# Alternating the two heads' 64-row products on TensorE, and another order of its pieces

## The chip, the cores and the metric

The kernel runs on one core of a Trainium2 chip. The metric is device time in microseconds (us) of one execution, the median of several runs. The core's engines are TensorE (PE in the profile, with its weight loads as PEld), VectorE (DVE), ScalarE (ACT), GpSimd (POOL) and SyncE (SP), which issues most DMAs.

## What is computed

One block on 512 tokens of width 1024: an RWKV-7 time mixer and a Mamba-2 (SSD) mixer side by side on one normed input, a gated merge, an output projection, and a mixture of 32 experts, two per token. Cut to its calls:

```python
h = rmsnorm(x, attn_norm_g[l])
proj = h @ w_in[l]
y_a = rwkv7_mix(p_rwkv, ...)    # 16 heads of 64, state 64x64 a head, scanned over tokens
y_b = ssd_mix(p_ssd, ...)       # 32 heads, chunks of 64
merged = g_a * (y_a @ w_up_rwkv[l]) + g_b * (y_b @ w_up_ssd[l])
x = x + merged @ w_out[l]
x = x + hier_moe(rmsnorm(x, ffn_norm_g[l]), ...)
return rmsnorm(x, final_norm_g)
```

The part that the change touches is inside `rwkv7_mix`, whose recurrence for one head is

```python
sa = jnp.einsum('bhij,bhj->bhi', state, -kk_t)
state = state * w_t[:, :, None, :] + sa[..., None] * (kk_t * a_t)[:, :, None, :] + v_t[..., None] * k_t[:, :, None, :]
y_t = jnp.einsum('bhij,bhj->bhi', state, r_t)
```

## The kernel before

The channels lie on the partitions, the 512 tokens along the free axis. The recurrence is computed in 8 chunks of 64 tokens, for two heads at a time: a *pair* has head 0 on partitions 0 to 63 and head 1 on 64 to 127. There are 8 pairs (`HP`).

Two phases come before the experts. In each, several *streams* (Python generators) are advanced by the function `drive` (line 266), which reads a string of the table `PLAN`: a letter advances one stream to its next `yield`, a number n issues n *pieces* of projections from a queue. A piece (lines 150 to 152) is three products of 128 rows by 512 columns; 8 pieces make one 128-column tile of the input projection. A tile's weights are split on their way into a high half (`wh`, ScalarE) and a low half (`wl`, VectorE, line 135), after a DMA from SyncE's queue; two tiles of each are held. TensorE's instructions stand in the program in the order in which these calls issue them, so the table fixes TensorE's order. The other engines' orders come from a scheduler that sees the same program.

The streams of the first phase are: a and b, the chains over chunks of even and odd pairs (`rwkv_chain`); c, their ends (`rwkv_tail`); d, a 32 by 32 inverse for each chunk (`rwkv_inverse`, 62 small VectorE instructions, lines 528 and 529, and TensorE pieces at lines 538, 550 and 560); e, what makes a pair's operands (`rwkv_front`); f, steps of the SSD. The second phase has one stream, the SSD's groups of heads (`ssd`), and the same kind of queue.

`rwkv_front` of one pair, as far as the change goes:

- Line 403 and 404: decay and `a` of the pair, each one product over 128 rows (`zst`) and one over 64 rows (`zlo`), into the banks `psw` and `psa`.
- Lines 475 to 481: GpSimd and VectorE make `LL` and `BK`, the left and right factors, a third of each for either head.
- Lines 486 to 502: for each head and each half of the chunks, four products of 64 rows by 128 columns into one bank, then three VectorE instructions (499 to 501) that mask them into `NB`, `LL` and `RB`, then a `yield`: four steps.
- Lines 504 to 511: for each head, eight transposes of 64 rows into one bank, one copy by ScalarE, a `yield`: two steps.

All these banks come from a ring of three (`rtile`, tag `rot`), which the other streams use too. A step that asks for a bank waits until the bank's last reader is done. The products are float32; each shows as two records in the trace, a transpose as one. A projection's products are float32r and show as one.

Behind the phases come the output projection, the router and the 32 experts, with 192 weight transfers of 1 MB each (6 an expert) through 18 buffers, which become free as the phases' pools close.

Of the kernel before, what the change touches and what calls it, by code (L numbers as in the profile page):

```python
# [14 lines left out]
AF = mybir.ActivationFunctionType  # L15
# [7 lines left out]
C = 64  # L23
NCK = T // C
# [15 lines left out]


PLAN = (
    "abcdef15e3e4e2e2e3e11e2e1e10ee8e1e2e1e1e1e1edeee4e1e2e2e2ee12ee9ee1e1dde1ddea1e1aedeee1ae3e1ae2e1a1ee2a1f2f2a2"
    "ee1a5a1e1eea2ae1dade2ddeabed3ab3baf3baff3ab2b1a4b1a2b1a2b2a2b2a1b1addb1dd2ab4aabc3b3a1b2a1bceecabeecc2bea3eb1a"
    "eee2be1a1b5ab2ebaee3b2ac3e1a1e2acec2cace2e1ae1edeeaee2e1ae3ee3aee3a5a2e2ee2a4ae1e1ae1edead2ddebaed3b1ac2b5b1c1"
    "b2eecbeecc1ee2b2ee1b1ee1b5b2ddbeee1dbd1a4ba3eab1e1bee1a1be2ae1bed1a1b4ba3b1a3b1a4b3ab5ab3a1bc6a2dad2adcdecebcc"
    "e1aeeb3ea1bee2aee1b5a2b1baeee3ab5eb1aeb1ea1eb1ae1be2ed1b1ac3b5b3bceeebccec1e2bee3e1b1ee2b5d1b2dbeee1dbd1a3b1ea"
    "b1e1ae1bce1ae1e1aed5ca1c1cac5a4a5a4a5a4a4add1dd1ab4ab4ba4ab5a1b2ba5ab4ab3ba5ab4abc4b4b5b2c1b1c1cbc5b3b2b7b4b4b"
    "5b3b5bc13c1ccc",
    "aa26aa7aaa5a2aa5a2aa4a2a24a2a1a7aa24aa5aaa4a2aa4a2aa3a2a33a2aa8aa26aa4a2aa3a2aa5a1a1a2a2a24a3aa5a1a25aa4a1aa4a"  # L50
    "2a1a3a2aa3a2a22a5aa5a3",
)

MU, W0, A0, KK, KA, RK, LNG, LNB, ATG, FFG, CVB = 0, 26, 34, 42, 50, 58, 66, 74, 82, 90, 98
# [3 lines left out]
def bcast(ap, dim, n):  # L58
    return ap.unsqueeze(dim).to_broadcast(list(ap.shape[:dim]) + [n] + list(ap.shape[dim:]))
# [3 lines left out]
def hybrid_block(ctx: ExitStack, tc: tile.TileContext, a, out):  # L63
    nc = tc.nc
    V, S, G, PE = nc.vector, nc.scalar, nc.gpsimd, nc.tensor
    PSUM = bass.MemoryType.PSUM

    def act(o, i, f, **kw):
        S.activation(o, i, f, **kw)  # L69
# [104 lines left out]
    def rtile(name="rt"):  # L174
        return rot.tile([128, 512], F32, name=name, tag="rot")
# [5 lines left out]
    with tc.tile_pool(name="first", bufs=1) as fp:  # L181
# [31 lines left out]
        for t in range(TT):  # L213
            n = (0, D, 0, D // 2)[t]
# [4 lines left out]
        ps = rtile()  # L219
# [4 lines left out]
        for k in range(KT):  # L224
            ps = rtile()
# [7 lines left out]
            if k == 4:  # L233
                ps = rtile()
# [6 lines left out]
                ps = rtile()  # L241
# [55 lines left out]
    zst = [rp.tile([128, T], F32R, name=f"zst{i}") for i in range(2)]  # L297
# [94 lines left out]
    def rwkv_front(hp):  # L392
# [6 lines left out]
        yield  # L399
        psw, psa = rtile(), rtile()  # L400
        for i, ps in enumerate((psw, psa)):
            rows = slice(64 * i, 64 * i + 64)
            PE.matmul(ps, wdw[:, i], zst[i], start=True, stop=False)
            PE.matmul(ps, wdw[rows, i], zlo[rows], start=False, stop=True)
        act(E1[:, :, 1:], c3(psw), AF.Sigmoid, bias=col(W0))
        av = f512("av")
# [6 lines left out]
        for g in range(3):  # L413
            ps = rtile()
# [7 lines left out]
            p3 = ps.rearrange("p (w n) -> p w n", n=128)  # L422
# [29 lines left out]
        ps = rtile()  # L452
# [13 lines left out]
        ps = rtile()  # L466
# [7 lines left out]
        bk = rp.tile([128, NCK, 3, C], F32, name="BK", tag="BK", bufs=1)  # L474
# [8 lines left out]
        yield  # L483
        NB = rp.tile([128, NCK, C], F32, name="NB", tag="NB", bufs=2)
        rb = rq.tile([128, 2, NCK, C], F32, name="RB", tag="RB", bufs=3)
        for e in range(2):
            rows = slice(64 * e, 64 * e + 64)
            krows = slice(64 - 64 * e, 128 - 64 * e)
            sl = slice(e, e + 2)
            ac, rc = (slice(0, 64), slice(64, 128)) if e == 0 else (slice(64, 128), slice(0, 64))  # L490
            for c4 in range(2):
                ps = rtile()
                p3 = ps.rearrange("p (c n) -> p c n", n=128)
                cr = slice(4 * c4, 4 * c4 + 4)
                for c in range(4):
                    cc = 4 * c4 + c
                    PE.matmul(p3[:, c], bk[rows, cc, sl].rearrange("p s t -> p (s t)"),
                              ll[rows, cc, sl].rearrange("p s t -> p (s t)"), start=True, stop=True)
                V.tensor_tensor(NB[rows, cr], p3[rows, :, ac], bcast(m_neg[rows], 1, 4), op=OP.mult)
                V.tensor_tensor(ll[krows, cr, 2 * e], p3[krows, :, ac], bcast(m_strict[krows], 1, 4), op=OP.mult)  # L500
                V.tensor_tensor(rb[:, e, cr], p3[:, :, rc], bcast(m_incl, 1, 4), op=OP.mult)
                yield
        bt = rq.tile([128, NCK, 128], F32, name="BT", tag="BT", bufs=3)
        for e in range(2):
            rows = slice(64 * e, 64 * e + 64)
            ps = rtile()
# [448 lines left out]
    with tc.tile_pool(name="op", bufs=2, side="right") as op:  # L955
# [111 lines left out]
        ps = rtile()  # L1067
# [238 lines left out]
    p = pend.pop()  # L1306
# [74 lines left out]
```

## Time and profile before

| | us |
|---|---|
| three runs, median (lowest, highest) | 1594.88 (1593.54, 1605.2) |
| the profiled execution, its own time | 1592.07 |
| its span, first to last instruction | 1590.4 |
| PE busy | 1472.9 (93%) |
| DVE busy | 901.8 (57%) |
| ACT busy | 683.4 (43%) |
| POOL busy | 256.2 (16%) |

The profile is one execution. TensorE's records are pipelined: one starts before the last has ended, so a busy TensorE isn't one at its peak, and the distance between starts tells more than a record's length. A matmul of full height and 512 columns in a projection shows 0.39 to 0.40 us and follows the one before by about 0.24. Waits are read from semaphores: "PE pin L152 <- DVE wl L135" is time in which TensorE's instruction at line 152, which writes `pin`, stood until VectorE's line 135 had written `wl`.

### The profile page before, as it was taken

Reading aid. Unit: us, or ns where it says so; the run is one execution under the profiler, and the core shown is the slowest. Engines: PE = TensorE matmul, PEld = TensorE weight load, DVE = VectorE, ACT = ScalarE, POOL = GpSimd, SP = SyncE. Lnnn points to the kernel's source line nnn. Section 1 sums busy time; section 2 is a strip of 40 time slices with the busy share of each in tenths; the row PEclk is TensorE's granted clock in tenths of the full one; section 3 lists DMA queues with packets and bytes.
Section 4 is the critical chain, followed back from the end, with each engine's and each line's share of the span. In section 5 each row is a group of like instructions: output and inputs, shape, how many; then the busy total and the mean of one; then the engine's idle time right before and its main releaser. Section 6 shows DMA issues by size and latency. Waiting matters only on the chain. (4 is left out here: it accounts for less than half of the span.)

```text
span 1590.4 us, 21601 instructions
## 1 busy us (share of the span) xinstructions
PE 1472.9 (93%) x8126; PEld 954.3 (60%) x8126; DVE 901.8 (57%) x1951; ACT 683.4 (43%) x1316; POOL 256.2 (16%) x241
## 2 busy tenths in 40 slices
PE   6988999999999999998998988898999999999995
PEld 4755766676766777766776766684444444444432
DVE  4688757887777844463666566433443443443334
ACT  6556556675656444536564644322211211211211
POOL 3121002211121000041414446101000000000001
PEclk9999899998999999999999999998999999999998
DMA  4311222111222324684665436875999999999891
GB/s 138 98 54 29 57 80 87 50 55 51 78 67 77 93 83 123 198 223 156 167 195 166 150 109 222 278 283 189 398 416 424 423 424 425 424 422 424 360 424 57
DMA packets 189136, 325.30 MB, mean 205 GB/s; under 512 B 11977, under 2 KB 147395, under 8 KB 163427
## 3 DMA queue, kind: packets, MB, share of 16 engines
q1 hardware_dynamic: 180131, 316.90, 55.2%
q0 software_dynamic: 2304, 4.20, 0.7%
q10 hardware_dynamic: 6592, 2.77, 0.6%
q8 instruction: 66, 1.08, 0.3%
q14 instruction: 43, 0.35, 0.1%
HBM read 306.99 MB, written 21.04 MB: 206 GB/s over the span
## 5 line engine op out<-in xcount | busy, mean ns | idle before, releaser
L150 PE MATMUL pin<-hh,wh 128*128 128x512 f32 x664 | 300.2, 452 | 9.3 <-ACT wh L69 5.3
L152 PE MATMUL pin<-hh,wl 128*128 128x512 f32 x664 | 270.1, 407 | 13.9 <-DVE wl L135 13.9
L151 PE MATMUL pin<-hl,wh 128*128 128x512 f32 x664 | 269.5, 406 | 0.8 <-DVE hl L230 0.8
L1185 PE MATMUL pgu<-we,xe 128*64 128x512 f32 x512 | 234.3, 600 | 0.0
L1186 PE MATMUL pgu<-we,xe 128*64 128x512 f32 x512 | 234.3, 600 | 0.0
L135 DVE TENSOR_TENSOR wl<-raw,wh 128x1024 fp32r<-128x1024 f32 x115 | 151.5, 1317 | 102.8 <-ACT wh L69 101.8
L69 ACT ACTIVATE wh<-raw 128x1024 fp32r<-128x1024 f32 x115 | 121.4, 1055 | 102.0 <-PE pin L151 82.8
L152 PEld LDWEIGHTS pin<-hh,wl 128*128 128x128 f32 x664 | 129.1, 194 | 49.2 <-DVE wl L135 18.4
L150 PEld LDWEIGHTS pin<-hh,wh 128*128 128x128 f32 x664 | 129.2, 195 | 47.1 <-issue 10.3
L151 PEld LDWEIGHTS pin<-hl,wh 128*128 128x128 f32 x664 | 130.1, 196 | 27.5 <-issue 5.4
L1185 PEld LDWEIGHTS pgu<-we,xe 128*64 128x64 f32 x512 | 66.5, 137 | 128.6 <-issue 124.2
L69 ACT ACTIVATE hid<-pgu,gsl 64x512 f32<-64x512 f32 x32 | 21.8, 682 | 280.0 <-PE pgu L1186 280.0
L1208 PE MATMUL pd<-we,hT 128*64 128x512 f32 x512 | 116.1, 592 | 1.2 <-DVE yy L1213 1.2
L150 PE MATMUL pin<-yh,wh 128*128 128x512 f32 x192 | 78.6, 409 | 8.5 <-ACT wh L69 3.5
L1192 DVE SCALAR_TENSOR_TENSOR hid<-pgu,gsl,hid 64x512 f32<-64x512 f32 x32 | 24.2, 757 | 106.0 <-ACT hid L69 106.0
L1208 PEld LDWEIGHTS pd<-we,hT 128*64 128x64 f32 x512 | 37.5, 137 | 73.8 <-issue 71.6
L1213 DVE TENSOR_TENSOR yy<-pd,yy 64x512 fp32r<-64x512 f32 x64 | 44.0, 688 | 63.8 <-ACT yy L69 62.7
L1228 DVE TENSOR_TENSOR x<-gps,x 128x512 f32<-128x512 f32 x128 | 78.1, 683 | 3.4 <-PE gps L1226 3.3
L1158 POOL DMA_INDIRECT xg<-x_d,at x16 | 16.2, 1012 | 387.2 <-DVE at L1148 384.8
L152 PE MATMUL pin<-yh,wl 128*128 128x512 f32 x192 | 76.4, 398 | 2.0 <-DVE wl L135 2.0
L69 ACT ACTIVATE yy<-pd 64x512 fp32r<-64x512 f32 x64 | 37.9, 592 | 89.9 <-PE pd L1208 89.0
L69 ACT ACT_TABLE_LOAD x54 | 69.3, 1283 | 16.3 <-issue 6.2
(367 smaller groups left out, 2597.4 us busy)
## 6 DMA issues: line engine op xcount, KB each, us to landing
we<-in_w_exp_gate_dram SPq DMA_DIRECT2D x64, 1024.0 KB
we<-in_w_exp_up_dram SPq DMA_DIRECT2D x64, 1024.0 KB
we<-in_w_exp_down_dram SPq DMA_DIRECT2D x64, 1024.0 KB
raw<-in_w_in_dram SPq DMA_DIRECT2D x83, 512.0 KB
lt<-acs_d SPq DMA_DIRECT2D x16, 512.0 KB
raw<-in_w_up_ssd_dram SPq DMA_DIRECT2D x16, 512.0 KB
xc_d<-cv SPq DMA_DIRECT2D x24, 256.0 KB
gt<-g_d SPq DMA_DIRECT2D x24, 256.0 KB
```

Of the source, the lines that this page charges most:

```text
L69: S.activation(o, i, f, **kw)
L135: V.tensor_tensor(lo, raw, hi.bitcast(F32), op=OP.subtract)
L150: PE.matmul(ps, wh[:, k, cs], xh[:, k], start=k == 0, stop=False)
L151: PE.matmul(ps, wh[:, k, cs], xl[:, k], start=False, stop=False)
L152: PE.matmul(ps, wl[:, k, cs], xh[:, k], start=False, stop=k == kt - 1)
L1158: G.indirect_dma_start(out=xg[p][0:n], out_offset=None, in_=x2_d, in_offset=bass.IndirectOffsetOnAxis(ap=at[0:n, p:p + 1], axis=0), bounds ...
L1185: PE.matmul(pgu[0:64], xe[k // 4][:, k % 4, ss_], wg[k // 4][:, k % 4], start=k == 0, stop=k == KT - 1)
L1186: PE.matmul(pgu[SR], xe[k // 4][:, k % 4, ss_], wu[k // 4][:, k % 4], start=k == 0, stop=k == KT - 1)
L1192: V.scalar_tensor_tensor(hid[SR], pgu[SR], gsl[SR], hid[SR], op0=OP.mult, op1=OP.mult)
L1208: PE.matmul(pd[i][64 * i:64 * i + 64], hT[:, k], wd[k // 2][:, k % 2, 512 * i:512 * i + 512], start=k == 0, stop=k == 3)
L1213: V.tensor_tensor(yy[i][rows, 1], src, yy[i][rows, 0].bitcast(F32), op=OP.subtract)
L1228: V.tensor_tensor(av, ps, av, op=OP.add)
```

## The change

It does three things.

1. In `rwkv_front`, the two full-height products of decay and `a` stand one after the other, then the two 64-row ones, instead of in turn.
2. The 64-row products of BK and LL are issued chunk by chunk for head 0 and head 1 in turn, into two banks: two steps of eight products and six VectorE instructions, instead of four of four and three. The transposes likewise: one step of sixteen into two banks, instead of two of eight.
3. Both strings of `PLAN` are others. They hold 564 and 339 pieces, as before, and the same number of each letter but e, which falls from 155 to 131 (three steps fewer for each of eight pairs). Most steps keep their place among the pieces or move by one to three.

```diff
 PLAN = (
-    "abcdef15e3e4e2e2e3e11e2e1e10ee8e1e2e1e1e1e1edeee4e1e2e2e2ee12ee9ee1e1dde1ddea1e1aedeee1ae3e1ae2e1a1ee2a1f2f2a2"
+    "abcdef15e3e4e2e5ee11e2e1e10ee8e3e2e1ed1eee4e3ee2e2ee10e2e9e1e1dd2ddea2aede1eeae2e1a3eea1ee4a1f2fa2ee1a6ae1ea2a1"
...
         psw, psa = rtile(), rtile()
         for i, ps in enumerate((psw, psa)):
+            PE.matmul(ps, wdw[:, i], zst[i], start=True, stop=False)
+        for i, ps in enumerate((psw, psa)):
             rows = slice(64 * i, 64 * i + 64)
-            PE.matmul(ps, wdw[:, i], zst[i], start=True, stop=False)
             PE.matmul(ps, wdw[rows, i], zlo[rows], start=False, stop=True)
...
-        for e in range(2):
-            rows = slice(64 * e, 64 * e + 64)
-            krows = slice(64 - 64 * e, 128 - 64 * e)
-            sl = slice(e, e + 2)
-            ac, rc = (slice(0, 64), slice(64, 128)) if e == 0 else (slice(64, 128), slice(0, 64))
-            for c4 in range(2):
-                ps = rtile()
-                p3 = ps.rearrange("p (c n) -> p c n", n=128)
-                cr = slice(4 * c4, 4 * c4 + 4)
-                for c in range(4):
-                    cc = 4 * c4 + c
-                    PE.matmul(p3[:, c], bk[rows, cc, sl].rearrange("p s t -> p (s t)"),
+
+        for c4 in range(2):
+            pss = [rtile(), rtile()]
+            cr = slice(4 * c4, 4 * c4 + 4)
+            for c in range(4):
+                cc = 4 * c4 + c
+                for e in range(2):
+                    rows, sl = slice(64 * e, 64 * e + 64), slice(e, e + 2)
+                    PE.matmul(pss[e][:, 128 * c:128 * c + 128], bk[rows, cc, sl].rearrange("p s t -> p (s t)"),
                               ll[rows, cc, sl].rearrange("p s t -> p (s t)"), start=True, stop=True)
+            for e in range(2):
...
                 V.tensor_tensor(NB[rows, cr], p3[rows, :, ac], bcast(m_neg[rows], 1, 4), op=OP.mult)
                 V.tensor_tensor(ll[krows, cr, 2 * e], p3[krows, :, ac], bcast(m_strict[krows], 1, 4), op=OP.mult)
                 V.tensor_tensor(rb[:, e, cr], p3[:, :, rc], bcast(m_incl, 1, 4), op=OP.mult)
-                yield
+            yield
         bt = rq.tile([128, NCK, 128], F32, name="BT", tag="BT", bufs=3)
+        pss = [rtile(), rtile()]
+        for c in range(NCK):
+            for e in range(2):
+                rows = slice(64 * e, 64 * e + 64)
+                PE.transpose(pss[e][:, 64 * c:64 * c + 64], bk[rows, c, e:e + 2].rearrange("p s t -> p (s t)"),
+                             ident[rows, rows])
         for e in range(2):
             rows = slice(64 * e, 64 * e + 64)
-            ps = rtile()
-            for c in range(NCK):
-                PE.transpose(ps[:, 64 * c:64 * c + 64], bk[rows, c, e:e + 2].rearrange("p s t -> p (s t)"),
-                             ident[rows, rows])
-            act(bt[:, :, rows], ps.rearrange("p (c n) -> p c n", n=C), AF.Copy)
-            yield
+            act(bt[:, :, rows], pss[e].rearrange("p (c n) -> p c n", n=C), AF.Copy)
+        yield
```

What moves on the engines is seen at three places. The line numbers of the changed kernel are one lower up to `rwkv_front` and differ by some lines inside it: 149 to 151 are the projection's products, 494 those of BK and LL, 509 the transposes, 401 and 404 decay and `a`, 541 and 553 the inverse's.

TensorE, the first pair's decay products, before:

```order
L152 MATMUL pin<-hh,wl 128x512
L403 MATMUL rt<-zst_304,wdw 128x512
L404 MATMUL rt<-zlo,wdw 128x512
L403 MATMUL rt<-zst_305,wdw 128x512
L404 MATMUL rt<-zlo,wdw 128x512
L150 MATMUL pin<-hh,wh 128x512
```

and in the changed kernel:

```order
L151 MATMUL pin<-hh,wl 128x512
L401 MATMUL rt<-zst_304,wdw 128x512
L401 MATMUL rt<-zst_305,wdw 128x512
L404 MATMUL rt<-zlo,wdw 128x512 x2
L149 MATMUL pin<-hh,wh 128x512
```

The two products over 64 rows (`zlo`), on rows 0 to 63 and 64 to 127, now follow each other.

TensorE, the second pair's products of BK and LL with the first pair's inverse (`TR`, `NB`) behind them, before (in the first row, two steps of four stand together):

```order
L497 MATMUL rt<-LL,BK 128x128 x8
L150 MATMUL pin<-hh,wh 128x512
L151 MATMUL pin<-hl,wh 128x512
L152 MATMUL pin<-hh,wl 128x512
L497 MATMUL rt<-LL,BK 128x128 x4
L150 MATMUL pin<-hh,wh 128x512
L151 MATMUL pin<-hl,wh 128x512
L152 MATMUL pin<-hh,wl 128x512
L538 MATMUL rt<-ident,TR 32x128 x8
L550 MATMUL rt<-TR,NB 32x32 x16
L497 MATMUL rt<-LL,BK 128x128 x4
```

and in the changed kernel:

```order
L494 MATMUL rt<-LL,BK 128x128 x8
L149 MATMUL pin<-hh,wh 128x512
L150 MATMUL pin<-hl,wh 128x512
L151 MATMUL pin<-hh,wl 128x512
L494 MATMUL rt<-LL,BK 128x128 x8
L149 MATMUL pin<-hh,wh 128x512
L150 MATMUL pin<-hl,wh 128x512
L151 MATMUL pin<-hh,wl 128x512
L541 MATMUL rt<-ident,TR 32x128 x8
L553 MATMUL rt<-TR,NB 32x32 x16
```

All sixteen products now stand ahead of the inverse, in two groups with one piece of projection between them, and each group fills two banks.

VectorE, the first pair's masks, before:

```order
L499 TENSOR_TENSOR NB<-rt,m_neg 64x256
L500 TENSOR_TENSOR LL<-rt,m_strict 64x4x64
L501 TENSOR_TENSOR RB<-rt,m_incl 128x256
L135 TENSOR_TENSOR wl<-raw,wh 128x1024
L499 TENSOR_TENSOR NB<-rt,m_neg 64x256
```

and in the changed kernel:

```order
L500 TENSOR_TENSOR NB<-rt,m_neg 64x256
L501 TENSOR_TENSOR LL<-rt,m_strict 64x4x64
L502 TENSOR_TENSOR RB<-rt,m_incl 128x256
L500 TENSOR_TENSOR NB<-rt,m_neg 64x256
L501 TENSOR_TENSOR LL<-rt,m_strict 64x4x64
L502 TENSOR_TENSOR RB<-rt,m_incl 128x256
L288 SCALAR_TENSOR_TENSOR r<-pin,vec_88,r 128x511
L134 TENSOR_TENSOR wl<-raw,wh 128x1024
```

Two banks are now emptied one behind the other, and the low half of a weight tile (`wl`) comes after both.

## Rows read from the trace of the kernel before

**Rows 1.** The page's busy tenths in 40 equal slices: TensorE, DMA engines.

```profile
PE   6988999999999999998998988898999999999995
...
DMA  4311222111222324684665436875999999999891
```

**Rows 2.** Busy us by stretch: length, PE, PEld, DVE, ACT, POOL, clock, DMA, GB/s.

```profile
30.00:645.00 615.00, 582.25 (x3764) 425.24 (x3763) 445.18 (x1194) 355.05 (x832) 82.92 (x82) 0.96 0.25 73
97.00:175.00 78.00, 65.29 (x439) 47.67 (x440) 68.82 (x194) 41.96 (x91) 17.00 (x14) 0.96 0.20 54
260.00:360.00 100.00, 93.85 (x588) 67.60 (x588) 85.34 (x243) 65.93 (x147) 18.75 (x23) 0.95 0.22 63
```

**Rows 3.** Timeline of TensorE, first pair: start us, us, engine, line, operation, tiles.

```profile
71.99 0.40 PE L151 MATMUL pin<-hl,wh 128*128 128x512 f32 x1
72.23 0.40 PE L152 MATMUL pin<-hh,wl 128*128 128x512 f32 x1
72.56 1.16 PE L497 MATMUL rt<-LL,BK 64*128 64x128 f32 x8
73.64 0.50 PE L150 MATMUL pin<-hh,wh 128*128 128x512 f32 x1
73.98 0.39 PE L151 MATMUL pin<-hl,wh 128*128 128x512 f32 x1
...
80.15 0.40 PE L152 MATMUL pin<-hh,wl 128*128 128x512 f32 x1
80.48 0.71 PE L508 MATMUL rt<-ident,BK 64*128 64x64 f32 x8
81.11 0.51 PE L150 MATMUL pin<-hh,wh 128*128 128x512 f32 x1
81.46 0.39 PE L151 MATMUL pin<-hl,wh 128*128 128x512 f32 x1
```

**Rows 4.** Timeline of TensorE around the first pair's decay products.

```profile
37.12 0.40 PE L152 MATMUL pin<-hh,wl 128*128 128x512 f32 x1
37.35 0.40 PE L403 MATMUL rt<-zst,wdw 128*128 128x512 f32 x1
37.68 0.50 PE L404 MATMUL rt<-zlo,wdw 64*128 64x512 f32 x1
...
38.96 0.51 PE L150 MATMUL pin<-hh,wh 128*128 128x512 f32 x1
39.30 0.39 PE L151 MATMUL pin<-hl,wh 128*128 128x512 f32 x1
```

**Rows 5.** Timeline of TensorE: products on parts of the array, inverse and experts.

```profile
122.86 1.32 PE L550 MATMUL rt<-TR,NB 32*32 32x32 f32 x32 [0.33 <-ACT TF L69]
...
126.08 0.69 PE L560 MATMUL rt<-TF,PB 32*32 32x32 f32 x32
...
1207.70 0.59 PE L1185 MATMUL pgu<-we,xe 128*64 128x512 f32 x1
1207.71 0.59 PE L1186 MATMUL pgu<-we,xe 128*64 128x512 f32 x1
```

**Rows 6.** Line 499's instructions (ns min/median/max) and its waits (us, times).

```profile
L499 DVE TENSOR_TENSOR NB<-rt,m_neg x32: 405/422/428, 73.8 to 522.4; 64x256 f32<-64x256 f32 x32
...
  PE rt L497: 12.8, 13
```

**Rows 7.** Waits of TensorE from 30 to 645 us: total, times, longest.

```profile
PE pin L152 <- DVE wl L135: 11.0, 5, 3.7
...
PE pin L150 <- DVE TI L529: 4.0, 1, 4.0
```

**Rows 8.** Timeline of GpSimd ahead of the first pair's products.

```profile
69.13 3.32 POOL L481 TENSOR_TENSOR BK<-av,E 64x512 f32<-64x512 f32 x2 [3.03 <-DVE av L479]
```

**Rows 9.** Waits of TensorE from 645 to 1000 us, the second phase.

```profile
PE rt L803 <- DVE y L818: 7.5, 7, 2.6
```

More of the change, by code (lines that the diff above doesn't have):

```diff
@@ L42 @@
 PLAN = (
-    "abcdef15e3e4e2e2e3e11e2e1e10ee8e1e2e1e1e1e1edeee4e1e2e2e2ee12ee9ee1e1dde1ddea1e1aedeee1ae3e1ae2e1a1ee2a1f2f2a2"
[L44 to L51, printed above, removed]
+    "abcdef15e3e4e2e5ee11e2e1e10ee8e3e2e1ed1eee4e3ee2e2ee10e2e9e1e1dd2ddea2aede1eeae2e1a3eea1ee4a1f2fa2ee1a6ae1ea2a1"
+    "dade2ddabed3ab3baf3baff3ab2b1a4b3ab1a2b2a1b1a2b1adbd1dd3ab4aabc3b4b2aa1bceecabeec2beca3eb1aeee2be1a1b5ab2ebae3e"
+    "b1ac5e1a2acec2cac2e1a1edeeaee2e1ae3ee1aee3a5ae4ee2a4ae2ae1d2ead2ddbaed3b1ac2b5b1c1b2e2ecbeecc1eeb2ee1b1ee1b5b2d"
+    "dbeee1dbd1ba4a3e2abbe1ab1e2a1bed1a1b4ba6ab3b1a3b3ab5ab3abc6a2dad2adcdecebcce1aeeb3ea1bee2aee1b5a2b1baee2e3ab4eb"
+    "ab1e1ab1ae1b2edb4acb5b3bc1eecebcec1e2bee3e1b1ee2b5d1b2dbeee1dbd2ea2b1ab2ae1bc1ae2a5edca1c1ca1ca9a5a3a6a3a5add1d"
+    "dab4ab4ab4ab5a1b2ba5ab4ab3ba5ab5abc4b4b5bcbc3cb1c5b3b2b7b4b4b5b3b5bc13c1ccc",
+    "aa26aa7aaa5aa2a5aaa4a1a24a5aa7aa24aa5aa1aa4a2a4a2aa3a2a33a2aa8aa26aa4a2aa3a2aa5a1aa3a1a24a4aa5a1a25aa5aaa4a3aa3"
+    "a2aa3a2a22a5aa5a3",
 )
@@ L485, in rwkv_front @@
         rb = rq.tile([128, 2, NCK, C], F32, name="RB", tag="RB", bufs=3)
-        for e in range(2):
-            rows = slice(64 * e, 64 * e + 64)
-            krows = slice(64 - 64 * e, 128 - 64 * e)
-            sl = slice(e, e + 2)
-            ac, rc = (slice(0, 64), slice(64, 128)) if e == 0 else (slice(64, 128), slice(0, 64))
-            for c4 in range(2):
-                ps = rtile()
-                p3 = ps.rearrange("p (c n) -> p c n", n=128)
-                cr = slice(4 * c4, 4 * c4 + 4)
-                for c in range(4):
-                    cc = 4 * c4 + c
-                    PE.matmul(p3[:, c], bk[rows, cc, sl].rearrange("p s t -> p (s t)"),
+        for c4 in range(2):
[6 more added lines that the diff above has]
+                    PE.matmul(pss[e][:, 128 * c:128 * c + 128], bk[rows, cc, sl].rearrange("p s t -> p (s t)"),
                               ll[rows, cc, sl].rearrange("p s t -> p (s t)"), start=True, stop=True)
+            for e in range(2):
+                p3 = pss[e].rearrange("p (c n) -> p c n", n=128)
+                rows, krows = slice(64 * e, 64 * e + 64), slice(64 - 64 * e, 128 - 64 * e)
+                ac, rc = (slice(0, 64), slice(64, 128)) if e == 0 else (slice(64, 128), slice(0, 64))
                 V.tensor_tensor(NB[rows, cr], p3[rows, :, ac], bcast(m_neg[rows], 1, 4), op=OP.mult)
```

## The prediction

> **What bounds the kernel now.** I read the busy slices of the page first. TensorE (PE) is busy at nine tenths or more in almost every slice, and the DMA engines fill up only in the last third, where the experts' weights stream [rows 1]. So the run has two stages: up to about 1000 us TensorE does the projections, and behind that the weight stream is full. The stream's first transfers stand behind the end of the two phases, so a microsecond taken from a phase moves the whole expert stage forward by one. The change touches only the phases.
>
> The first phase is that of the RWKV streams. From 30 to 645 us TensorE is busy for 582.25 of 615 us, so some 33 us are left in which it stands [rows 2]. The reader should see that this is not even: in 97 to 175 us VectorE (DVE) is busy 68.82 of 78 us and TensorE only 65.29, so there VectorE's program sets the pace; in 260 to 360 us it has 85.34 of 100 [rows 2]. Elsewhere TensorE is ahead of every other engine, and what it saves is time. The waits say the same: the dearest of the first phase are for VectorE, 11.0 us in five for the low halves of weights (the longest 3.7), and the longest single one, 4.0 us, falls while VectorE works through the inverse [rows 7].
>
> **The change part by part.** A plain projection product starts 0.24 us after the one before it, 71.99 to 72.23 [rows 3]; I take 0.235. What a group of other products costs is then read from the starts of the projections around it.
>
> *Products of BK and LL (line 497).* The group of four at 72.56 stands between L152 at 72.23 and the second next projection at 73.98 [rows 3]. Two projections alone would take 0.47, so the group costs 1.75 - 0.47 = 1.28 us. It shows as 8 records, two for each product, 1.08 us from its first start to the next projection, 0.135 each. Four such groups for a pair of heads are 5.12 us. The change issues two groups of 8 products, head 0 and head 1 in turn, on rows 0 to 63 and 64 to 127 of the array, into two banks. If the halves run side by side, a group still costs 1.28 and a pair 2.56: saved 2.56. If they run in single file, a group is 8 x 0.135 = 1.08 longer, 2.36, and a pair 4.72: saved 0.40, the two entries and exits that fall away.
>
> *Transposes of BK (line 508).* The same reading from 80.15 to 81.46 gives 1.31 - 0.47 = 0.84 us for 8 [rows 3], 1.68 a pair. Side by side 16 cost 0.84: saved 0.84. In single file another 8 x 0.079 (0.63 us for 8) = 0.63, together 1.47: saved 0.21.
>
> *The decay products (lines 403 and 404).* Four products from L152 at 37.12 to the projection at 39.30 cost 2.18 - 0.47 = 1.71 us, and the three steps from 37.68 to 38.96 show 0.43 each where height changes every time [rows 4]. Now the two full-height ones stand together and then the two 64-row ones: 0.235 + 0.235 + 0.33 + 0.43 + 0.34, with the last product beside the third, less 0.47, is 1.10: saved 0.61. In single file 0.43 more: saved 0.18.
>
> Side by side that is 2.56 + 0.84 + 0.61 = 4.01 us a pair and 32 us for eight pairs; in single file 0.79 and 6.3 us. Which of the two, no row shows outright, since nothing in the trace pairs row halves at full width. The nearest rows differ. Line 560 alternates row blocks of 32 with 32 columns: 32 records in 0.69 us, about 0.02 each or 0.6 ns a column, against 0.135/128, or 1.05 ns, in line 497; line 550 has the same shape and 1.32 us, no gain [rows 5]. They differ in the moving operand: 550 reads every eighth element, 560 and the changed products read contiguous columns. Column halves do run side by side: lines 1185 and 1186 start 0.01 us apart at 0.59 us each [rows 5]. I take side by side.
>
> The Trainium skill ("TensorE: Matmul & The Clock Gate", Part 3, "Measured speedup vs the span model") states that products on different row groups span one product's time plus about 4 ns a tile. By it the sum is the 32 us; line 560 agrees, line 550 does not [rows 5].
>
> *What is behind the new groups.* VectorE empties a bank with three instructions of 0.42 us [rows 6], 1.27 us, so 2.5 us for a new group. It waited 12.8 us in thirteen waits for these products [rows 6], so it gets its work sooner: that helps. Against it, a group takes two of the ring's three banks, and the second group needs the bank that the first three instructions free. That is a wait of 0 (VectorE prompt, two projections between) up to VectorE's lateness; the longest waits for it now are 4.0 and 3.7 us [rows 7]. I take nothing as a cost of its own and let it decide how much of the saving passes (below).
>
> *POOL.* The first group now needs the second head's part of BK too, the second of two instructions. In the first pair both end at 69.13 + 3.32 = 72.45, and the group starts at 72.56 [rows 8, 3]: no cost there. At worst it is one instruction, 1.66 us, in each pair, 13 us. I take nothing, because POOL had ended before the first product even here, where the gap is smallest.
>
> *The order of the pieces.* Both plans hold as many projections as before, 564 and 339, and all calls of the streams but the 24 that fell away. Steps move by one to three projections, 0.7 to 2.1 us. This could take away or double the waits that it meets: up to 33 us of standing in the first phase [rows 2], and in the second the 7.5 us in seven waits of line 803 among them [rows 9]. The moves are small and not mostly at those waits, so I take nothing, with 8 us to either side in the range. On SyncE's queue (SP) about a dozen weight loads change places with a store beside them by one or two rows. The DMA share of the phase is 0.25 [rows 2], so the transfers themselves have room; a load that comes late behind a store would show as one more wait like that of 3.7 us [rows 7], and is inside the 8 us.
>
> **How much passes.** Two of the eight pairs have their products where VectorE sets the pace (97 to 175 us); there I let all be lost. Two more lie in 260 to 360 us; there half. So 5/8 of 32 = 20 us pass. The profiled execution took 1592.07 us (1590.4 of span and 1.7 around it): 1572. The median of the three runs, 1594.88, is 2.8 above it: 1575.
>
> **The rivals.**
> *A, single file:* the halves don't overlap. For it speaks line 550, against it 560 and 1185/1186 [rows 5]. Saved 6.3 x 5/8 = 4: 1591.
>
> *B, the banks hold it back:* two groups with one projection between them (0.70 us) last 2 x (1.28 + 0.70) = 3.96 us, while VectorE needs 5.06 for their evictions. TensorE stands 1.1 us a pair, 8.8 in all: 20 - 8.8 = 11 saved, 1584. Before, four groups took 7.9 us against the same 5.06, so nothing waited. Against it: where a second projection stands between (as in the first pair), the groups take longer than the evictions. The Trainium skill ("TensorEngine Tiling (Array Packing)", "PSUM Bottleneck") says the same: tiling speeds TensorE up and not the emptying of PSUM. The trace agrees in the 0.42 us of an eviction, which the change leaves alone [rows 6].
>
> *C, slower:* VectorE is late at both later places of each pair, the second group and the transposes. If TensorE met a wait like the 3.7 us one [rows 7] at each, that is 8 x (7.4 - 4.0) = 27 us more: 1622. It decides from 4.0 us of new waits in a pair. Against it: these two lines of waits hold six such waits in the whole first phase [rows 7], not sixteen.
>
> *D, the new order also removes waits:* a third of the 33 us on top: 1564.
>
> **How the numbers follow.** Forecast (1563 to 1584 with its unknown moves) 0.60; A 0.12; B 0.18; C 0.06; D 0.04. 1575 is the forecast's. The range 1562 to 1592 holds the forecast, A, B and D, and leaves out C and the tails, under 2 in 10. A change of 1%, 16 us, is about what a measurement of this kernel can tell from none: faster (under 1579) takes D, most of the forecast and a little of B, 0.60; slower (over 1611) is C, 0.06; the rest, 0.34, is within 1%.
>
> **What would show it.** In the changed profile a group of 8 products of BK and LL, 16 records, should last about 1.2 us; 2.2 means single file. Its projection should follow within 1.3 us. The transposes, 16 in one group, about 0.7. Everything behind the first phase should look as now and come some 20 us earlier. New waits of TensorE for VectorE's NB or RB at the second group would be B or C. I am wrong if line 497's groups shrink and the phase does not, because the waits for low halves of weights grow by the same.

## The result, and the profile after

The changed kernel took 1578.99 us (median of four runs, 1575.03 to 1583.86) against 1594.21 us of the kernel before in the same runs: ratio 0.9894, interval 0.9855 to 0.9932, so 15 to 17 us faster. A second series gave 0.9886, 0.9861 to 0.9911.

| | us |
|---|---|
| the profiled execution, its own time | 1579.57 |
| its span | 1577.9 |
| PE busy | 1446.3 (92%) |
| DVE busy | 901.4 (57%) |
| ACT busy | 681.8 (43%) |
| POOL busy | 256.6 (16%) |

The page's busy slices of the changed kernel, TensorE and DMA engines, which answer to [rows 1]:

```profile
PE   6978999899999999989998988898999999999995
...
DMA  4321132222222333764665527875999999999891
```

TensorE has lost 26.6 us of busy time, ScalarE 1.6 and the others next to nothing. The stages are as before: TensorE to about 1000 us, then the weight stream.

The new group of products, in the timeline of the changed kernel (start, us, engine, line, tiles), which answers to [rows 3]:

```profile
74.24 0.40 PE L151 MATMUL pin<-hh,wl 128*128 128x512 f32 x1
74.57 1.16 PE L494 MATMUL rt<-LL,BK 64*128 64x128 f32 x16
75.66 0.51 PE L149 MATMUL pin<-hh,wh 128*128 128x512 f32 x1
76.00 0.39 PE L150 MATMUL pin<-hl,wh 128*128 128x512 f32 x1
```

Sixteen records take the 1.16 us that eight took, and the next projection follows the group's start by 1.09. By the reading that the prediction used, from 74.24 to 76.00 less 0.47, the group costs 1.29 us. The halves run side by side.

The decay products, which answer to [rows 4], and the first pair's transposes:

```profile
37.80 0.40 PE L151 MATMUL pin<-hh,wl 128*128 128x512 f32 x1
38.04 0.62 PE L401 MATMUL rt<-zst,wdw 128*128 128x512 f32 x2
38.59 0.50 PE L404 MATMUL rt<-zlo,wdw 64*128 64x512 f32 x2
39.02 0.50 PE L149 MATMUL pin<-hh,wh 128*128 128x512 f32 x1
39.35 0.40 PE L150 MATMUL pin<-hl,wh 128*128 128x512 f32 x1
...
79.96 0.27 PE L509 MATMUL rt<-ident,BK 64*128 64x64 f32 x1
81.44 0.68 PE L509 MATMUL rt<-ident,BK 64*128 64x64 f32 x15 [1.22 <-DVE RB L502]
82.05 0.50 PE L149 MATMUL pin<-hh,wh 128*128 128x512 f32 x1
```

From 37.80 to 39.35 less 0.47 the decay products cost 1.08 us. The transposes need 0.6 us from 81.44 to the next projection, for twice as many as before, but only after 1.22 us of waiting for their second bank, which VectorE had not emptied.

Where the time came from is seen when both programs are laid side by side by their projection pieces. The table gives the start of a piece's last product in the changed kernel less that in the kernel before, worked out from the records of both traces:

| piece | start before, us | changed less before, us |
|---|---|---|
| 40 | 53.1 | +2.0 |
| 120 | 157.5 | +4.3 |
| 220 | 299.2 | +7.4 |
| 260 | 364.1 | -0.2 |
| 300 | 413.3 | -5.8 |
| 340 | 472.4 | -8.3 |
| 380 | 531.2 | -11.3 |
| 420 | 574.9 | -15.4 |
| 540 | 677.4 | -15.4 |
| 560 | 707.5 | -10.0 |
| 919 | 1064.7 | -12.4 |

Five of the eight pairs have their products of BK and LL before piece 260 (in 73 to 320 us), three behind it. The first five brought nothing in this execution, the last three all of it. The windows of both stretches (length, PE, PEld, DVE, ACT, POOL, clock, DMA share, GB/s), first two rows before, then two of the changed kernel:

```profile
30.00:364.10 334.10, 309.63 (x1945) 224.73 (x1944) 257.12 (x689) 205.58 (x456) 57.89 (x59) 0.95 0.22 64
364.10:677.40 313.30, 305.02 (x1970) 226.53 (x1969) 202.56 (x524) 167.13 (x397) 30.00 (x26) 0.97 0.33 98
```

```profile
30.00:364.00 334.00, 294.94 (x1948) 213.97 (x1947) 256.57 (x692) 203.75 (x454) 53.14 (x58) 0.94 0.22 64
364.00:662.00 298.00, 289.70 (x1969) 216.84 (x1968) 201.52 (x522) 167.74 (x399) 34.90 (x28) 0.98 0.34 103
```

In the first stretch TensorE is busy 14.7 us less in the same time: it stands 39.1 us instead of 24.5. In the second it stands 8.3 us in both, and the 15.3 us that it is busy less are 15.3 us of time. The products of three pairs save 11.5 us of work (worked out further below); the rest goes with the clock, of which this stretch has 10 us at 1.2 GHz instead of 19. The waits of the changed kernel's TensorE from 30 to 364 us (total, times, longest):

```profile
PE cb L581 <- DVE SV L602: 6.4, 3, 4.5
PE pin L151 <- DVE wl L134: 6.0, 3, 2.3
PE rt L453 <- ACT kk L68: 5.7, 3, 2.4
PE rt L494 <- DVE RB L502: 4.3, 3, 3.3
PE rt L467 <- DVE tmp L462: 4.1, 3, 1.7
...
PE rt L419 <- DVE v L288: 1.8, 1, 1.8
...
PE rt L509 <- DVE RB L502: 1.2, 1, 1.2
```

Against [rows 7], where all of the waits of lines 150 and 152 lie in this stretch, the waits for low halves fell from 11.0 to 6.0. But a dozen others are new or longer, spread over the chains' states (`SV`), the front's own inputs (`kk`, `v`) and the banks (`RB`): 25 us in all, of which VectorE ends 15 and ScalarE 10.

### The profile page after: what moved, and what is told of

It is laid out like the page before. It is cut to its first block, busy times and chain, and to the rows that moved or that the text cites. A ratio compares the mean times of both kernels' runs of the same rounds, so it can differ in the third digit from the quotient of the medians.

```text
span 1577.9 us, 21594 instructions
## 1 busy us (share of the span) xinstructions
PE 1446.3 (92%) x8126; PEld 938.0 (59%) x8126; DVE 901.4 (57%) x1951; ACT 681.8 (43%) x1316; POOL 256.6 (16%) x241
## 3 DMA queue, kind: packets, MB, share of 16 engines
q8 instruction: 66, 1.08, 0.3%
## 5 line engine op out<-in xcount | busy, mean ns | idle before, releaser
L149 PE MATMUL pin<-hh,wh 128*128 128x512 f32 x664 | 297.3, 448 | 3.2 <-ACT wh L68 1.6
L151 PEld LDWEIGHTS pin<-hh,wl 128*128 128x128 f32 x664 | 129.3, 195 | 43.5 <-DVE wl L134 12.5
L149 PEld LDWEIGHTS pin<-hh,wh 128*128 128x128 f32 x664 | 129.2, 195 | 40.7 <-issue 7.9
L149 PE MATMUL pin<-yh,wh 128*128 128x512 f32 x192 | 79.4, 414 | 8.0 <-ACT wh L68 3.2
L1161 POOL DMA_INDIRECT xg<-x_d,at x16 | 16.2, 1009 | 387.3 <-DVE at L1151 384.8
L150 PE MATMUL pin<-yl,wh 128*128 128x512 f32 x192 | 76.5, 398 | 0.1
```

Of the source, the lines that this page charges most:

```text
L149: PE.matmul(ps, wh[:, k, cs], xh[:, k], start=k == 0, stop=False)
L150: PE.matmul(ps, wh[:, k, cs], xl[:, k], start=False, stop=False)
L151: PE.matmul(ps, wl[:, k, cs], xh[:, k], start=False, stop=k == kt - 1)
L1161: G.indirect_dma_start(out=xg[p][0:n], out_offset=None, in_=x2_d, in_offset=bass.IndirectOffsetOnAxis(ap=at[0:n, p:p + 1], axis=0), bounds ...
```

## The experiments

All ran beside the kernel before. Their profiles are compared in three stretches, by the pieces again: 12 to 260, 260 to 540 (the rest of the first phase), 540 to 919 (mostly the second phase). Each cell has the length in us, then TensorE's idle time, then the time at the lower clock level (1.2 GHz), worked out from the records and the granted clock:

| kernel | ratio | 12 to 260 | 260 to 540 | 540 to 919 |
|---|---|---|---|---|
| before | 1 | 333.3; 24.5; 35 | 313.2; 8.3; 19 | 387.3; 38; 24 |
| changed | 0.9894 | 332.5; 39.1; 38 | 298.1; 8.3; 10 | 390.2; 38; 31 |
| f1 changed again | 0.9886 | 328.7; 39.5; 24 | 298.0; 8.3; 10 | 390.4; 37; 34 |
| e1 head by head | 0.9922 | 333.9; 31.0; 41 | 299.7; 8.8; 3 | 389.3; 36; 38 |
| e2 both old strings | 0.9914 | 331.9; 36.1; 37 | 304.0; 10.7; 14 | 390.8; 40; 31 |
| e3 old second string | 0.9880 | 334.0; 38.7; 38 | 300.6; 8.0; 17 | 381.5; 32; 20 |
| g1 the same again | 0.9885 | 331.7; 35.6; 41 | 297.8; 9.1; 7 | 386.5; 36; 27 |
| g2 old first string | 0.9916 | 331.0; 36.1; 33 | 304.1; 10.5; 15 | 388.2; 36; 31 |
| f2 VectorE work early | 0.9948 | 341.6; 43.5; 41 | 298.1; 8.3; 10 | 392.4; 36; 41 |
| f3 VectorE work late | 0.9904 | 330.8; 36.8; 34 | 302.1; 12.8; 7 | 390.8; 37; 34 |
| e4 a third of wl on GpSimd | 0.9987 | 334.2; 37.2; 41 | 305.7; 12.4; 17 | 395.4; 40; 38 |
| f4 pieces into the waits | 1.0055 | 324.6; 37.7; 61 | 332.2; 22.5; 24 | 387.7; 36; 27 |

Behind piece 919 these executions take 525.2 to 525.7 us, but g1, f2 and e4 take 529.5 to 529.7; why isn't shown.

The clock has a part in these times. At 1.2 GHz a projection product follows the one before by 0.43 us instead of 0.235, as here in the kernel before, where the level fell at 107.1 us, in a wait of 4 us:

```profile
107.61 0.77 PE L150 MATMUL pin<-hh,wh 128*128 128x512 f32 x1 [3.97 <-DVE TI L529]
108.17 0.63 PE L151 MATMUL pin<-hl,wh 128*128 128x512 f32 x1
108.60 0.63 PE L152 MATMUL pin<-hh,wl 128*128 128x512 f32 x1
```

The mean granted clock of each execution gives its time at 1.2 GHz: twice what it lacks to 1, times the span. The kernel before took 1586.38 us in an execution with a granted clock of 0.973 and 1603.71 in one with 0.959. Over 131 executions, each set against the mean of its own kernel, a microsecond more at 1.2 GHz goes with 0.38 us more of time. This is an estimate, and it says what goes together, not which causes which. The kernel before has 115 us at 1.2 GHz on average (54 executions), the changed one 104 (10): some 4 us of the 18 between their means go with the clock, and 13.6 are left. The two profiled executions, both at a granted clock of 0.968, lie 12.5 us apart. Below, "at equal clock" means set to the same time at 1.2 GHz by this estimate.

### Head by head (e1_single_file)

The grouping into two banks stays, but within a group head 0's products come first, then head 1's; the transposes likewise.

```diff
-            for c in range(4):
-                cc = 4 * c4 + c
-                for e in range(2):
+            for e in range(2):
+                for c in range(4):
+                    cc = 4 * c4 + c
```

> The changed kernel (1579.0 us) with its steps, its banks and its order of pieces, but within a step head 0's products stand first and then head 1's, for the products of BK and LL and for the transposes (the decay products stay as changed). Theory 1 (the halves run side by side, and that is where the gain comes from): a group of 8 products of BK and LL lasts about 2.2 us instead of 1.16, the 16 transposes about 1.3 instead of 0.7; 16 x 1.08 + 8 x 0.63 = 22 us more work of TensorE. Up to the 260th piece of projection, where the change gained nothing, it costs little; of the last three pairs all 8 us come through. 1587 to 1592. Rival (the gain is the new order of pieces): within 3 us of the changed kernel.

Measured 1582.3 us, ratio 0.9922 (0.9894 to 0.9950). Timeline of e1:

```profile
76.10 0.40 PE L151 MATMUL pin<-hh,wl 128*128 128x512 f32 x1
76.43 1.71 PE L494 MATMUL rt<-LL,BK 64*128 64x128 f32 x16
78.07 0.50 PE L149 MATMUL pin<-hh,wh 128*128 128x512 f32 x1
...
79.67 1.08 PE L509 MATMUL rt<-ident,BK 64*128 64x64 f32 x16
80.68 0.50 PE L149 MATMUL pin<-hh,wh 128*128 128x512 f32 x1
```

The time lies between the two expectations, 3.3 us above the changed kernel. The group takes 1.71 us, not 1.16 and not the 2.2 of single file: even so the two halves overlap in part, and TensorE has about 11 us more work instead of the expected 22. The starts of the 16 records, in ns after the first, show how:

```
0 213 325 436 548 554 660 767 771 879 883 990 1102 1214 1325 1437
```

The record that releases head 0's bank is the one at 883. By that and by the distances, head 0's eight are 0, 213, 325, 436, 548, 660, 771 and 883; head 1's begin at 554, beside head 0's fifth, with the same 213 to their second, and end at 1437. So three of head 1's records started ahead of the last of head 0's. In the changed kernel all sixteen go in pairs, 7 ns apart, a pair every 112 ns behind the first.

The Trainium skill ("TensorE: Matmul & The Clock Gate", Part 3, "The mechanism") says that products start and end in program order, without reordering, and that weight loads are pulled ahead of running products. The starts of e1 don't agree: across the two row halves, three records of the later head begin before the earlier head's last.

The kernel before holds the same thing, and I had missed it. Its plan lets two steps stand together in three places. Timeline of before:

```profile
116.32 2.05 PE L497 MATMUL rt<-LL,BK 64*128 64x128 f32 x16
118.30 0.51 PE L150 MATMUL pin<-hh,wh 128*128 128x512 f32 x1
...
164.01 1.71 PE L497 MATMUL rt<-LL,BK 64*128 64x128 f32 x16
...
379.56 2.05 PE L497 MATMUL rt<-LL,BK 64*128 64x128 f32 x16
381.53 0.51 PE L150 MATMUL pin<-hh,wh 128*128 128x512 f32 x1
```

At 116 and 379 the two steps are of one head, on the same rows: 2.05 us, single file. At 164 they are the second of head 0 and the first of head 1, on different rows: 1.71 us, as in e1, with a start again 6 ns behind another. This row told the two cases apart before any run.

The run also shows what TensorE's own work is worth in each stretch. From its first start to the projection behind it a group needs 0.55 us more than in the changed kernel (1.64 against 1.09 where nothing disturbs it), a pair's transposes 0.30 more (0.94 against 0.64), worked out from the records: 7.0 us up to piece 260 and 4.2 behind it. Up to piece 260 the stretch is 1.4 us longer, and TensorE stands 31.0 us instead of 39.1: next to nothing passes. Behind it the stretch is 1.6 us longer with 7 us less at 1.2 GHz, 4.2 at equal clock: all of it passes.

### Both old strings (e2_old_order)

The alternation with the strings of `PLAN` before, with the e's of the merged steps taken out.

```diff
-    "abcdef15e3e4e2e5ee11e2e1e10ee8e3e2e1ed1eee4e3ee2e2ee10e2e9e1e1dd2ddea2aede1eeae2e1a3eea1ee4a1f2fa2ee1a6ae1ea2a1"
+    "abcdef15e3e4e2e2e3e11e2e1e10ee8e3e2e2edeee4e1e2e2e2ee12ee9e1e1dd1ddea2aedeee1ae3e1ae2e1a1ee2a1f2f2a2ee1a5a1e1e"
...
```

> The changed kernel with both strings of the plan as before, only without the 24 letters of the steps that fell away (the second and fourth step of products, the second of transposes). Theory 1 (side by side): most of the gain is there without the new order, 1576 to 1584. Rival (the order of pieces gives the gain): about 1590 or more. A third view, that the new order brought the 14.6 us of added waits before the 260th piece: under 1575.

Measured 1584.57 us, ratio 0.9914 (0.9884 to 0.9945), just above the range of Theory 1. Most of the gain needs no new order. TensorE's idle time up to piece 260 is 36.1 us here too, so the new waits there come from the faster products and not from moved steps.

### The strings one at a time (e3_old_second_phase, g1_old_second_again, g2_old_first_new_second)

e3 and g1 are one kernel: the new first string, the second phase's old one. g2 has the old first string and the new second.

```diff
-    "aa26aa7aaa5aa2a5aaa4a1a24a5aa7aa24aa5aa1aa4a2a4a2aa3a2a33a2aa8aa26aa4a2aa3a2aa5a1aa3a1a24a4aa5a1a25aa5aaa4a3aa3"
-    "a2aa3a2a22a5aa5a3",
+    "aa26aa7aaa5a2aa5a2aa4a2a24a2a1a7aa24aa5aaa4a2aa4a2aa3a2a33a2aa8aa26aa4a2aa3a2aa5a1a1a2a2a24a3aa5a1a25aa4a1aa4a"
+    "2a1a3a2aa3a2a22a5aa5a3",
```

> The changed kernel with the second phase's string as before. In the profiles the changed kernel was 15.4 us ahead at the first phase's last pieces and 12.4 at the end, so the second phase gave back 3 us. If its new order does that: about 1576. If it is the state in which the second phase starts: 1579, with the same waits at line 806 and 813.

> The changed kernel with the second phase's order string of the kernel before, again, in more rounds (it had 1576.0 us, ratio 0.988, its interval overlapping the changed kernel's 0.989). If the new string of the second phase gives about 3 us back: ratio 0.986 to 0.988, and the second phase (from the 540th projection piece on) near 381 to 385 us against 390 of the changed kernel. If the two strings of the second phase are worth the same and the earlier difference was clock: 0.989 to 0.990 and 387 to 390 us there.

> The changed kernel with the first phase's order string of the kernel before (pieces of the second products left out where the change merges them) and the new string of the second phase: the fourth corner beside changed (1579), old strings both (1584.6) and old second string alone (1576). If the strings add up: 1584.6 + 3 = about 1587 to 1588, ratio 0.993. If the new first string is worth nothing and the difference between those runs was clock: about 1579 to 1582, ratio 0.990.

Measured 1576.03 us (0.9880, 0.9839 to 0.9922), 1577.65 us (0.9885, 0.9855 to 0.9916) and 1582.95 us (0.9916, 0.9891 to 0.9942). Four series with the new first string lie at 0.9880 to 0.9894, two with the old one at 0.9914 and 0.9916. Weighted by their intervals that is 0.9886 against 0.9915: the new first string is worth 4.6 us, give or take about 4. At equal clock, with 20 executions of the new one (changed, f1, e3, g1) against 13 of the old, it is 3.5, give or take 1.5. In the traces it shows from piece 260 to 540: 304.0 and 304.1 us with the old one, 297.8 to 300.6 with the new. At equal clock the stretch is 7.1 and 7.4 us shorter than before with the old string and 10.7 to 11.7 with the new.

g1 fell between its two expectations, and so did g2. The second string isn't seen in the times: 0.9914 old and 0.9916 new beside the old first string. In the traces the last stretch is 388.2 to 390.4 us with the new one in these kernels and 381.5 to 390.8 with the old, so e3's short 381.5 was in part an execution with little time at 1.2 GHz. The new string does lose time at the head of the second phase: against before, 3.6 and 5.4 us from piece 540 to 560 (f1, changed), where the old one loses 0.2 and 1.1 (g1, e2); some of that comes back later. Whether it costs a few us in all stays open.

### VectorE work early and late (f1_changed_again, f2_added_vector_early, f3_added_vector_late)

f1 is the changed kernel, as the measure of the two others on the same chip. f2 adds to VectorE thirty subtractions into a tile that nobody reads, two behind the low half of every other weight tile from the 4th to the 33rd (up to piece 260). f3 adds the same thirty between the 34th and the 63rd.

```diff
         V.tensor_tensor(lo, raw, hi.bitcast(F32), op=OP.subtract)
+        if 4 <= wn[0] <= 33 and wn[0] % 2:
+            junk = rp.tile([128, kt // 2, src.shape[-1]], F32, name="junk", tag="junk", bufs=1)
+            for i in range(2):
+                half = hi.bitcast(F32)[:, i * kt // 2:(i + 1) * kt // 2]
+                V.tensor_tensor(junk, half, half, op=OP.subtract)
```

> The changed kernel itself once more, for comparison with the three beside it on the same chip: 1579, as before. The old string of the second phase alone (1576.0 in four runs) is then either beside it or 3 us ahead.

> The changed kernel with 20 us of VectorE work added before the 260th piece: two more subtractions of 128x512 (0.68 us each) into a tile nobody reads, behind every second weight tile from the 4th to the 33rd. Theory 1 with its reason (before the 260th piece VectorE's program sets the pace): that stretch grows from 332.5 us by 8 to 20, and the time to 1587 to 1599. Rival (the pace there is set by something else, latencies of the chains or ScalarE): VectorE's 77 us of room take it up, the stretch grows by less than 4 us, 1579 to 1583.

> The same additions behind every second weight tile from the 34th to the 63rd, so in the 298 us behind the 260th piece, where TensorE is busy for 290 and VectorE for 202. Theory 1: TensorE sets the pace there, so the stretch grows by less than 4 us: 1579 to 1583. Rival (VectorE's order matters as much there): 8 to 20 us more.

Measured 1579.48 us (f1), 1589.74 (f2; ratio 0.9948, 0.9930 to 0.9966) and 1581.81 (f3; 0.9904, 0.9870 to 0.9938). The added work in f2 and in f3 (line, engine, tiles, busy us, mean ns, idle before):

```profile
L142 DVE TENSOR_TENSOR junk<-wh 128x512 f32<-128x512 f32 x30 | 22.5, 750 | 0.1
```

```profile
L142 DVE TENSOR_TENSOR junk<-wh 128x512 f32<-128x512 f32 x30 | 22.4, 746 | 0.2
```

The same 22 us add 10.3 us to the time of f1 where they stand up to piece 260, and 2.3 us behind it, which the intervals don't tell from nothing. Both times lie where Theory 1 had them. But f2 has 116 us at 1.2 GHz on average, f3 102, the changed kernel 104. At equal clock the work adds 6.5 and 4.0 us, and the five executions of f3 don't tell these apart. The stretches say the same: f2's first one is 6.5 to 8 us longer than those of f1 and the changed kernel at equal clock, f3's second one 5.3. Window of f2 and of f3, the stretch in which each has the work:

```profile
30.00:364.00 334.00, 291.85 (x1881) 211.65 (x1880) 266.55 (x711) 197.14 (x436) 52.31 (x54) 0.94 0.23 63
```

```profile
364.00:662.00 298.00, 285.16 (x1917) 212.78 (x1917) 212.32 (x546) 164.91 (x396) 31.40 (x27) 0.99 0.34 102
```

So up to 364 us VectorE's program passes on nearly a third of what is put into it at equal clock, and about half with the clock, though it is busy only 77% of that stretch (256.57 of 334.00 in the changed kernel): a share below 1 doesn't make added work free. Behind 364 us it passes on a fifth or so. These two runs don't show that the stretches differ in what VectorE's work is worth; e1 shows that they differ in what TensorE's is.

### A third of the low halves on GpSimd (e4_pool_low_halves)

Meant to relieve VectorE: every third subtraction of a low half, up to the 81st tile and so in both phases, goes to GpSimd, 27 in all.

```diff
-        V.tensor_tensor(lo, raw, hi.bitcast(F32), op=OP.subtract)
+        (G if wn[0] % 3 == 0 and wn[0] < 84 else V).tensor_tensor(lo, raw, hi.bitcast(F32), op=OP.subtract)
```

> The changed kernel with the low half of every third weight tile of the first phase computed by GpSimd instead of VectorE, 28 of 83 tiles; the same values. It takes 28 x 1.3 = 36 us of work from VectorE. Theory 1 with its reason (up to the 260th piece VectorE's program sets the pace): the 25 us of TensorE's waits for VectorE there shrink by 5 to 15 us: 1564 to 1574. Rival (those waits come from fixed distances in the order, or GpSimd's own queue is late with the tiles): no change or slower, 1579 to 1590.

Measured 1595.6 us, ratio 0.9987 (0.9961 to 1.0013): the whole gain is lost, more than either view expected. By line, engine and tiles (busy us, mean ns):

```profile
L137 POOL TENSOR_TENSOR wl<-raw,wh 128x1024 fp32r<-128x1024 f32 x27 | 64.7, 2397 | 233.8 <-ACT wh L68 183.4 <-DVE TI L535 31.9 <-PE rt L544 13.9
...
L137 DVE TENSOR_TENSOR wl<-raw,wh 128x1024 fp32r<-128x1024 f32 x88 | 118.2, 1343 | 77.5 <-ACT wh L68 77.3 <-issue 0.2
```

A low half takes 2.40 us on GpSimd against 1.34. TensorE's waits for low halves grow from 10.7 to 16.7 us up to 1030 us, 6.6 of them for GpSimd's (the longest, 4.2 us, is for one of VectorE's). Another 5 us of the 16 go with the clock (117 us at 1.2 GHz); the rest is open. As a test of VectorE's part it decides nothing, since it adds a wait of its own; f2 and f3 do that.

### Pieces into the waits (f4_filled_waits)

37 pieces are taken from the later part of the first phase and put ahead of 18 steps at which TensorE waited, to fill the 39 us. The second string is the old one, so e3 and g1 are what it is to be compared with.

```diff
-    "abcdef15e3e4e2e5ee11e2e1e10ee8e3e2e1ed1eee4e3ee2e2ee10e2e9e1e1dd2ddea2aede1eeae2e1a3eea1ee4a1f2fa2ee1a6ae1ea2a1"
+    "abcdef15e3e7e2e5ee11e2e1e12ee8e3e4e1ed1eee4e3ee2e4ee11e2e9e5e1dd2ddea2aede1eeae2e1a3eea4ee4a1f2fa2ee1a6ae1ea2a"
...
```

> The changed kernel with the second phase's string as before and 37 pieces of projection moved in the first phase: put ahead of the 18 steps where TensorE waited longest (before lines 419, 453, 467, 494, 581), taken from between the last steps. Theory 1: before the 260th piece TensorE has 39 us to spare, and pieces put there cost nothing, so the phase ends 10 to 20 us sooner: 1560 to 1570. Rival (the streams' steps come later by as much as is put ahead of them, or the last steps, now closer, wait for each other): 1576 or slower.

Measured 1605.07 us, ratio 1.0055 (1.0027 to 1.0084): slower than before. Waits of its TensorE, first from 30 to 364 us, then from 364 to 700 us:

```profile
PE pin L149 <- DVE TI L532: 7.9, 2, 6.7
PE pin L151 <- DVE wl L134: 5.6, 3, 4.4
PE pin L149 <- DVE v L288: 5.4, 2, 4.7
```

```profile
PE rt L541 <- DVE TR L534: 6.3, 3, 3.0
PE pin L149 <- ACT wh L68: 3.9, 2, 2.5
```

A piece isn't TensorE's alone. It brings its weight's split and its eviction, and these stand in the queues of engines that TensorE already waits for: up to 364 us TensorE waits 22 us at a piece's first product (L149), 1.5 in the changed kernel. Piece 260 comes 8 us earlier, but the streams are further behind by then, and the pieces that were moved are missing later: from piece 260 to 540 the phase is 34 us longer than in the changed kernel. From piece 12 to 540 TensorE stands 60 us, 47 in the changed kernel, and has 85 us at 1.2 GHz against 48. Over all executions f4 has 140 us at that level against 102 of e3 and g1, so by the estimate about half of its 27 us go with the clock.

## Why the prediction was right, and where it was not

The forecast was 1575 us; 1579 came out, inside the range and on the predicted side. Its steps:

**Side by side: right, and to be had from the trace.** A group was to cost 1.28 us and cost 1.29. The sentence "Which of the two, no row shows outright" was wrong: the row at 164.01 us of before showed two row halves overlapping at full width, and those at 116 and 379 what single file is. Rival A falls with it; and even the head-by-head order of e1 isn't rival A, since it keeps part of the overlap. Its step of 0.135 us a record was an average with the exit in it; the records stand 0.112 apart.

The Trainium skill ("TensorE: Matmul & The Clock Gate", Part 3, "Measured speedup vs the span model") gives about 4 ns for a further tile; the trace has 7 ns between the two of a pair, and agrees in what follows.

**The 32 us: nearly right.** Worked out from the records, from a group's first start to the projection behind it: products took 26 groups x 1.08 + 2 x 1.98 + 1.64 = 33.7 us before; sixteen undisturbed groups of 1.09 are 17.4. With 13 entries and exits fewer, 0.2 each, 18.9 us are saved instead of 20.5: three of the 32 groups that I counted already stood against another. Transposes: 16 x 0.64 less 8 x 0.64, and 1.6 for entries and exits, 6.7 as forecast. Decay: 1.61 less 0.98, 0.63 against 0.61. Together 30.6 us of TensorE's work.

**How much passes: the sum came out, the places did not.** 5/8 of 32, 20 us, was to pass, with two pairs lost in 97 to 175 us and half of two in 260 to 360: 8 us from the five pairs ahead of piece 260 and 12 from the three behind it. The two series gained 15 to 18, some 4 of which go with less time at 1.2 GHz, which I had no term for. Five pairs, 19 us of the 30.6, lie before piece 260, and there the four executions with the new first string gained 0.8 us (changed), 4.6 (f1) and 1.6 (g1) or lost 0.7 (e3). Three pairs, 11.5 us, lie behind it, and there 12.6 to 15.4 us were gained, 10.7 to 11.7 at equal clock: all of it, nearly as counted. The step that failed is the reading of VectorE's busy share: I took 0.88 of a window for VectorE's pace, 0.85 for half, and everything else for TensorE's. The whole stretch up to 364 us, where VectorE is busy 0.77, passes on next to nothing of what TensorE saves or, in e1, has to do more; that holds for the first pair too, which I had counted in full. That the total fits is luck: the 8 us that did not come from the first five pairs were made up in part by the clock.

**The order of the pieces: not nothing.** It was taken as 0, with 8 us to either side. The new first string gains about 4 us: 4.6 by the ratios, which barely separate it from nothing, 3.5 at equal clock, and the stretch behind piece 260 shows 4. With the old one about 4 of the 11.5 us of the last three pairs don't pass, and the time is 8 to 10 us above the forecast (g2, e2) instead of 4.

**The banks: rival B in part.** It was to cost 1.1 us in every pair, 8.8. The trace has 4.3 us in three waits at the second group and 1.2 at the transposes, 5.5 together; twelve of sixteen groups ran undisturbed in 1.09 to 1.16. The price is not a matter of the two groups and their evictions: it falls where VectorE is busy with something else. The dearest one, in the timelines of TensorE and VectorE of the changed kernel:

```profile
116.30 0.48 PE L494 MATMUL rt<-LL,BK 64*128 64x128 f32 x2
120.13 2.04 PE L494 MATMUL rt<-LL,BK 64*128 64x128 f32 x14 [3.34 <-DVE RB L502]
```

```profile
116.30 1.23 DVE L134 TENSOR_TENSOR wl<-raw,wh 128x1024 fp32r<-128x1024 f32 x1
117.44 0.16 DVE L532 TENSOR_TENSOR TI<-TI,tm 128x8 f32<-128x8 f32 x1
117.52 0.74 DVE L288 SCALAR_TENSOR_TENSOR r<-pin,vec,r 128x511 f32<-128x511 f32 x1
118.18 0.62 DVE L534 STREAM_TRANSPOSE TR<-TI 128x256 f32<-128x256 f32 x1
118.73 0.38 DVE L500 TENSOR_TENSOR NB<-rt,m_neg 64x256 f32<-64x256 f32 x1
```

The first group had filled its banks by 115.5 us, but its masks stand on VectorE behind the end of the first pair's inverse, a low half and a shift, until 118.73. Rival C saw this, with too many of them: 27 us at sixteen places, and there were four waits.

**What I took as nothing and was.** POOL's second instruction: TensorE waited 0.7 us in two waits for `BK`, against the 13 us of the bound. SyncE's queue: the waits for `wl` fell from 11.0 to 6.0 us. VectorE got its products sooner: line 499, 500 in the changed kernel, waits 5.9 us for them instead of the 12.8 of [rows 6] (the last row; the first two are what line 494 itself waited for):

```profile
  DVE RB L502: 4.3, 3
  POOL BK L481: 0.7, 2
...
  DVE NB L500: 5.9, 5
```

**What would have shown me wrong** was that line 497's groups shrink and the phase does not. That is what happened up to piece 260, not by the low halves, whose waits shrank, but by a dozen new or longer waits for other things, 15 us for VectorE's and 10 for ScalarE's, the longest single one 4.5 us.

That TensorE's saving turned into waiting there is shown by the windows and by e1. What sets the pace there instead is shown in part only: work added to VectorE passes for nearly a third (f2), but for a fifth or so behind piece 260 too (f3), so VectorE alone doesn't explain why TensorE's saving passes in one stretch and not in the other. The part of ScalarE and of the streams' own chains is argued from the names of the waits and was not tested.

## What to carry to other kernels

Where two operations stand side by side by chance somewhere in the trace, that row is better evidence on whether they overlap than any likeness of shapes: look for it first. What a saving on the busiest engine is worth is read from how the stretch answers to that engine and its neighbours, and not from a neighbour's busy share: where VectorE was busy 0.77 of the time, next to nothing of TensorE's saving passed. Work put back on the busiest engine, as in e1, reads this directly. The time at the lower clock belongs beside every difference of a few us. And a wait can't be filled with work that needs the very engine that is waited for.

## What was not expected of the hardware

- Products of 64 rows on different halves of the array overlap even when all of one half's are issued first: 16 records in 1.71 us, between 1.16 (in turn) and 2.05 (same rows), with products of the second half starting before the last of the first.
- A group of such products has an entry and an exit of some 0.1 us each beyond a projection's 0.235 (0.33 from 74.24 to 74.57, 0.34 from 75.66 to 76.00), so groups that stand together pay without any overlap: the two steps at 116 us of before took 1.98 us to the next projection, where two apart take 1.08 each and 0.2 more in entry and exit.
- The same kernel's executions differ in where TensorE falls to 1.2 GHz. The window from 30 to 364 us of f1, which is the changed kernel's program and whose row stands in the first section:

```profile
30.00:364.00 334.00, 294.51 (x2010) 213.56 (x2009) 257.37 (x696) 207.26 (x465) 56.33 (x59) 0.96 0.23 66
```

  At a mean clock of 0.94 the changed kernel shows 1948 matmul records in it, f1 at 0.96 shows 2010, and reaches piece 260 4.8 us earlier. Ahead of the falls stand TensorE's waits of 1 to 4.5 us or the inverse's small products. A comparison of single profiles to a few us says nothing here unless the time at 1.2 GHz is set against it.
